# The attention gate's sums moved beside the convolutions, the feed forward gate's into its first projection

## The chip, the cores and the metric

One Trainium2 chip; the kernel runs on one core of it. The metric is the device time of one execution in microseconds (us). The core's engines are TensorE (PE, with its weight loads as PEld), VectorE (DVE), ScalarE (ACT), GpSimd (POOL) and SyncE (SP). Each engine runs its own instructions in a fixed order and waits on semaphores where an operand isn't ready; SP, ACT and POOL also issue DMAs.

## The reference

A transformer block for 512 tokens of width 2048 whose shifts, scales and gates come from a vector c through one wide weight (adaptive layer norm). Cut to what matters here:

```python
sh_a, sc_a, g_a, sh_f, sc_f, g_f = split(silu(c) @ ada_w + ada_b, 6)   # six rows of 2048
h = modulate(rms_norm(x, norm_mix), sh_a, sc_a)
...                                                # convolutions and attention -> y (512 x 2048)
x = x + g_a * (y @ w_out)                          # the output projection, gated
h = modulate(rms_norm(x, norm_ffn), sh_f, sc_f)
x = x + g_f * ((silu(h @ ffn_w1) * (h @ ffn_w3)) @ ffn_w2)
```

g_a is the attention's gate and g_f the feed forward's. Each is 2048 numbers, each number a product of c with a column of ada_w (2048 x 12288, float32).

## The kernel before

**The sums.** A row such as g_a is computed on DVE, 512 columns at a time. ada_w's 2048 rows lie as 16 tiles of 128 partitions x 512 columns (256 KB each). `ada` (L184) goes over them: it loads tiles (L195, on SP), and for each adds tile times one number per partition to a running sum `acc` (L201, one scalar_tensor_tensor). For the gates `acc` starts at zero (L190, a memset on POOL) with the bias in its first partition (L191, a DMA on SP). Then `quarters` (L219) sums `acc` over the partitions with four small matmuls, and the row goes to DRAM by `row_of` (L228, a DMA on POOL), to `gad` for the attention's gate and `gfd` for the feed forward's. `ada_bcast` (L230) does this and loads the row back to all 128 partitions as the tile `ga`. `ffn_part` (L466) computes one 512-column part of what the feed forward needs: parts 0 to 7 are its shifts and scales, 8 to 11 its gate.

**Where the sums stand.** `gates_beside` (L1002) yields the tiles that run beside the convolutions: parts 3 to 10, then the first 512 columns of g_a, nine parts of 16 tiles. The output projection (y @ w_out) is done in four blocks of 512 output columns. A block is eight steps; a step loads a tile of w_out (`raw`, L91, on SP), splits it into a high part `whi` (L92, ACT) and a low part `wlo` (L93, DVE), and makes 24 matmuls with it (L110 to L112, three for each product), six into each of four PSUM tiles of 128 tokens. `beside_block` (L1075) runs beside each block: it sends the block's gate through `ada_bcast`, and computes the next block's 512 columns of g_a (beside the last block, part 11, the last of g_f). `residual` (L1092) closes a block: for each of the four PSUM tiles t = tile times gate (L1096), x2 = x2 + t (L1097), a square on ACT (L1098), and DMAs of the result on POOL (L1102). L1096 empties the PSUM tile, and the next block's first matmul into it waits for that. `after_taken` lets the sums of a block be issued only after the residual's last add.

**The feed forward's first projection** multiplies by w1 and w3 in products of a Strassen-like scheme, one unit of 128 columns in seven products, after two plain units (`NP8` = 8 products). For every product a weight tile is split (`w_hi` L1237 on ACT, `w_lo` L1244 on DVE), multiplied on PE (L1251, L1253) and added to its outputs on DVE (L1258, L1262). Some weight tiles are sums of two (L1349 on DVE, or a DMA on POOL that adds while it loads, L1227, onto what a DMA on SP brought, L1225). The main loop goes over `order`, the list of products, and prepares later ones ahead.

**The order on an engine** isn't that of the code: a scheduler places each instruction by its operands and its own estimate of times, so an instruction without open dependencies may be placed far ahead of where it is written. Once built, an engine's order is fixed.

Of the kernel before, what the change touches and what calls it, by code (L numbers as in the profile page):

```python
# [9 lines left out]
F32 = mybir.dt.float32  # L10
# [3 lines left out]
ALU = mybir.AluOpType  # L14
# [3 lines left out]
P = 128  # L18
D = 2048
S = 512  # L20
NT = S // P
KC = D // P
# [47 lines left out]
def block_kernel(ctx: ExitStack, tc: tile.TileContext, a: dict, out: bass.AP):  # L70
    nc = tc.nc
# [4 lines left out]
    def pool(name, bufs=1, stack=ctx, **kw):  # L76
        return stack.enter_context(tc.tile_pool(name=name, bufs=bufs, reuse_waits="tile", **kw))
# [61 lines left out]
    accp = pool("acc", 2)  # L139
# [9 lines left out]
    cT = cp.tile([P, KC], F32, name="cT")  # L149
# [3 lines left out]
    aring = pool("araw", 8, stack=st0)  # L153
# [29 lines left out]
    ada_v = ada_w.rearrange("(p k) n -> p k n", k=KC)  # L183

    def ada(ring, width, c0, n, got, bias=False):

        acc = accp.tile([P, 512], F32, tag="acc", name="acc")[:, :n]
        step = min(width // n, KC)
        if bias:
            nc.gpsimd.memset(acc, 0.0)  # L190
            nc.sync.dma_start(acc[0:1, :], a["ada_b"][:, c0:c0 + n])  # L191
        for k0 in range(0, KC, step):
            raw = ring.tile([P, width], F32, tag="araw", name="araw")
            rv = raw[:, :step * n].rearrange("p (k n) -> p k n", k=step)
            nc.sync.dma_start(rv, ada_v[:, k0:k0 + step, c0:c0 + n])  # L195
            for k in range(k0, k0 + step):
                w, s = rv[:, k - k0, :], cT[:, k:k + 1]
                if k == 0 and not bias:
                    nc.vector.tensor_scalar(acc, w, s, None, op0=ALU.mult)
                else:  # L200
                    nc.vector.scalar_tensor_tensor(acc, w, s, acc, op0=ALU.mult, op1=ALU.add)  # L201
            yield
        got.append(acc)
# [15 lines left out]
    def quarters(t):  # L219

        ps = aux()
        for j in range(4):
            nc.tensor.matmul(ps[32 * j:32 * j + 32, :P], ones[:, 0:32], t[:, j * P:(j + 1) * P], start=True, stop=True,
                             skip_group_check=True)
        return ps[:, :P]

    def row_of(row, t):
        nc.gpsimd.dma_start(row.rearrange("o (j t) -> (o j) t", j=4), t[0:P:32, :P])  # L228

    def ada_bcast(row, small, dst, acc):  # L230

        nc.scalar.copy(small, quarters(acc))
        row_of(row, small)
        nc.gpsimd.dma_start(dst, row.to_broadcast([P, 512]))
# [225 lines left out]
    gfd = dram.tile([1, D], F32, name="gfd")  # L460
    gad = [dram.tile([1, 512], F32, name=f"gad{n}") for n in range(4)]
    rsd = [dram.tile([1, S], F32, name=f"rsd{c}") for c in range(8)]

    def ffn_part(ring_, width, j):

        got = []  # L466
        if j < 8:
            m, j = 1 - j % 2, j // 2
            yield from ada(ring_, width, (3 + m) * D + j * 512, 512, got)
            ada_cols(aux, got[0], 1, m, 4 * j, 4)  # L470
        else:
            cs = slice((j - 8) * 512, (j - 7) * 512)
            yield from ada(ring_, width, 5 * D + cs.start, 512, got, bias=True)
            nc.scalar.copy(got[0][:, :P], quarters(got[0]))
            row_of(gfd[:, cs], got[0])
        yield

    def ffn_parts(ring_, width, js):
        for j in js:
            yield from ffn_part(ring_, width, j)  # L480
# [60 lines left out]
    for name, m, t0, t1, n in (("q", 0, 0, NT, P), ("c", 1, NT, NT + 1, NP_), ("s", 2, 0, NT, P), ("w", 3, 0, NT, P)):  # L541
        f = SCALE if name == "q" else 1.0
        for h in range(2):
# [6 lines left out]
                                           op0=ALU.mult, op1=ALU.mult)  # L550
# [437 lines left out]
        for c in range(8):  # L988
            yield from conv(c)

    acc_g = []

    class Places:
        n = 0
# [5 lines left out]

    def gates_beside():
        places = Places()  # L1002
        yield from ffn_parts(places, 512, range(3, 11))
        yield from ada(places, 512, 2 * D, 512, acc_g, bias=True)

    later = gates_beside()
    weave(beside(convs(), later, (0.4,) * 24 + (0.83,)), attention_steps(), 0.59 / 3)
# [20 lines left out]
    gst = ExitStack()  # L1028
    gp = pool("ga", 1, stack=gst)
    xp = pool("x2", 2, stack=gst)  # L1030
    tp = pool("tmp", 2, stack=gst)
    aring = pool("aring2", 3, stack=gst)
    keep = pool("keep", 1, stack=gst)
    ss2 = gp.tile([P, NT, 4], F32, name="ss2")
    x2s = [None] * 4
# [27 lines left out]
        x2s[n] = xp.tile([P, NT, 512], F32, tag="x2", name="x2")  # L1063
        nc.sync.dma_start(x2s[n], x[:, n * 512:(n + 1) * 512].rearrange("(i p) n -> p i n", p=P))

    taken = [None]

    def after_taken(side):
        while True:
            with tc.issue_after(taken[-1]) if taken[-1] else ExitStack():  # L1070
                if next(side, side) is side:
                    return
            yield

    def beside_block(n, ga):  # L1075

        own = acc_g[-1]
        side = ffn_part(aring, 1024, 11)
        if n < 3:
            side = ada(aring, 1024, 2 * D + (n + 1) * 512, 512, acc_g, bias=True)  # L1080
        for t, _ in enumerate(after_taken(side)):
            if t == 0:
                if n:
                    x2_turned(n - 1)
                ada_bcast(gad[n], tp.tile([P, P], F32, tag="dg", name="dg"), ga, own)
                if 0 < n < 3:
                    x_load(n + 1)
            if n == 0 and t in (2, 5):
                x_load(t // 3)
            yield  # L1090

    def residual(n, ga, pst, tiles):  # L1092
        for i in tiles:
            t = tp.tile([P, 512], F32, tag="t", name="t")
            x2 = x2s[n][:, i, :]
            nc.vector.tensor_mul(t, pst[i], ga)  # L1096
            taken[-1] = nc.vector.tensor_add(x2, x2, t).ins  # L1097
            nc.scalar.activation(t, x2, AF.Square, accum_out=ss2[:, i, n:n + 1])  # L1098
        for i in tiles[::2]:
            to = xd[n] if n < 2 and i else \  # L1100
                out[0, i * P:(i + 2) * P, n * 512:(n + 1) * 512].rearrange("(i p) n -> p i n", p=P)
            nc.gpsimd.dma_start(to, x2s[n][:, i:i + 2, :])  # L1102
# [76 lines left out]
    for n in range(4):  # L1179
        ga = tp.tile([P, 512], F32, tag="ga", name="ga")  # L1180
# [238 lines left out]
    for u in range(PLAIN, NU):  # L1419
# [9 lines left out]
        else:  # L1429
            order += new[2:-1]  # L1430
            late = new[-1]

    begun = set()

    def begin(u):
# [23 lines left out]
    for n in range(3):  # L1459
        prepare(n, "split")  # L1460
    for n, s in enumerate(order):
        for m in range(n + 5, n + 1, -1):
            if m < len(order) and lead[id(order[m])] == m - n:
                prepare(m, "sum")
        if n == 0:
            for m in range(5, NP8):
                order[m]["load"]()
        for m in (n + 6, n + 7) if n < NP8 else (n + 7,):
            if m < len(order) and (n >= NP8 or m < NP8 + 1):
                begin(order[m]["u"])  # L1470
        if n > 2:
            prepare(n + 2, "split")
            h_sums(n)
        if n == len(order) - 5:
            zst.close()
            krp = pool("kraw", 1, side="right")
            for half in range(2):
                k_load(0, half)
        if n == 2:
            second_half()  # L1480
            h_sums(0)
        s["mm"](s)
        if n == 2:
            prepare(3, "split")
            h_sums(2)
            prepare(4, "split")
            with tc.issue_after(hi_ins[-1]):
                shifted(8, 8)
                shifted(0, 8)
        if n + 1 < len(order):  # L1490
            s["post"](s)
# [262 lines left out]
```

## Time and profile before

| | |
|---|---|
| three runs | 2167.26, 2167.44, 2171.16 us, median 2167.44 |
| profiled execution, its own time | 2169.3 us |
| its span | 2167.5 us |
| granted TensorE clock | 0.999 |

The times below come from the profiled execution, counted from the start of its span. The convolutions and the attention come first, the output projection lies from about 686 to 872 us, the first projection of the feed forward from 871 to about 1740, and the second from there to the end. A row of a timeline gives the start and the duration in us, the engine, the line, the operation, output and inputs with their shapes, how many were joined into the row, and in brackets the idle time ahead of it with what ended that. In a row of groups the bar is followed by the busy time in us, the mean duration of one in ns, and the idle time ahead of the group.

### The profile page before, as it was taken

The numbers are of one execution on the slowest core, as the hardware profiler recorded it, in microseconds if no ns is written. First come the engines' busy times: TensorE is split into PE (matmuls) and PEld (weight loads), VectorE is DVE, ScalarE is ACT, GpSimd is POOL, SyncE is SP. The second block draws the span as 40 slices with busy tenths as digits, with TensorE's granted clock in tenths as the row PEclk, the third lists the DMA queues.
The fourth block names the chain that finished last, engine by engine and source line by source line (L and its number), as shares of the span: only waits on it lengthen the run. The fifth ranks groups of instructions, "written<-read, shape, count | busy, mean of one in ns | idle before, by whom it ended". The sixth has DMA issues, their size and how long they took to land.

```text
span 2167.5 us, 30927 instructions
## 1 busy us (share of the span) xinstructions
PE 2137.4 (99%) x11501; PEld 1792.0 (83%) x11501; DVE 1720.6 (79%) x2562; ACT 1004.2 (46%) x1613; POOL 222.5 (10%) x273
## 2 busy tenths in 40 slices
PE   7999999999999999999999999999999999999999
PEld 5778778788788888888888888888888887888887
DVE  6788779877876656988878887888788887878788
ACT  5325244555555223744444444444444455444543
POOL 2310000000000100000000000000000122111210
PEclk9999999999999999999999999999999999999999
DMA  9975768745644975397777777777776499797975
GB/s 353 363 238 167 248 198 272 224 146 158 182 142 149 307 266 171 93 230 181 173 189 173 170 172 181 177 174 167 177 184 167 112 302 288 147 305 140 287 159 142
DMA packets 442219, 437.61 MB, mean 202 GB/s; under 512 B 20420, under 2 KB 349164, under 8 KB 441428
## 3 DMA queue, kind: packets, MB, share of 16 engines
q1 hardware_dynamic: 373088, 326.71, 48.2%
q0 software_dynamic: 68448, 108.44, 24.2%
q8 instruction: 90, 1.47, 0.3%
q14 instruction: 61, 0.50, 0.1%
q10 hardware_dynamic: 532, 0.48, 0.1%
HBM read 415.61 MB, written 19.96 MB: 201 GB/s over the span
## 4 chain that ended last, share of the span: by engine, by line
PE 88%; DVE 5%; DMA 5%; issue 1%; ACT 1%; SPq 0%; POOL 0%; DVEq 0%; ACTq 0%
PE main L1251 15%; PE aux L1251 11%; PE aux L1609 9%; PE main L1609 9%; PE main L1253 8%; PE main L110 7%; PE main L112 6%; PE main L111 6%; PE aux L1253 6%; DMA araw<-in_ada_w 2%; PE aux L110 2%; PE aux L112 2%; PE aux L111 2%; PE aux L902 2%; DVE acc L201 1%
## 5 line engine op out<-in xcount | busy, mean ns | idle before, releaser
L1237 ACT CAST whi<-raw 128x1024 fp32r<-128x1024 f32 x246 | 257.7, 1047 | 286.4 <-PE main L1251 95.7
L1251 PE MATMUL main<-hC,whi 128*128 128x512 f32 x1408 | 353.5, 392 | 1.4 <-ACT whi L1237 1.4
L1237 ACT CAST whi<-t 128x1024 fp32r<-128x1024 f32 x186 | 195.3, 1051 | 263.3 <-PE aux L1251 70.3
L1244 DVE TENSOR_TENSOR wlo<-raw,whi 128x1024 fp32r<-128x1024 f32 x218 | 265.9, 1220 | 54.5 <-ACT whi L1237 52.1
L1251 PEld LDWEIGHTS main<-hC,whi 128*128 128x128 f32 x1408 | 253.3, 189 | 47.6 <-ACT whi L1237 1.6
L1251 PE MATMUL aux<-hC,whi 128*128 128x512 f32 x1072 | 268.9, 392 | 0.0
L1251 PEld LDWEIGHTS aux<-hC,whi 128*128 128x128 f32 x1072 | 192.9, 189 | 34.4
L1253 PEld LDWEIGHTS main<-hC,wlo 128*128 128x128 f32 x1408 | 192.0, 190 | 13.6
L1253 PE MATMUL main<-hC,wlo 128*128 128x256 f32 x1408 | 196.4, 282 | 0.0
L110 PE MATMUL main<-alo,whi 128*128 128x512 f32 x444 | 179.7, 405 | 0.7 <-DVE rq L564 0.7
L112 PE MATMUL main<-ahi,whi 128*128 128x512 f32 x444 | 174.0, 393 | 0.0
L111 PE MATMUL main<-ahi,wlo 128*128 128x512 f32 x444 | 173.8, 391 | 0.0
L92 ACT CAST whi<-raw 128x1024 fp32r<-128x1024 f32 x70 | 73.6, 1052 | 189.9 <-PE main L112 122.7
L1253 PEld LDWEIGHTS aux<-hC,wlo 128*128 128x128 f32 x1072 | 146.3, 190 | 10.4
L1253 PE MATMUL aux<-hC,wlo 128*128 128x256 f32 x1072 | 149.7, 282 | 0.0
L1581 DVE TENSOR_TENSOR wlo<-t,whi 128x1024 fp32r<-128x1024 f32 x102 | 124.2, 1220 | 29.1 <-ACT whi L1237 29.0
L1227 POOL DMA_DIRECT2D t<-in_ffn_w x42 | 64.9, 1546 | 794.6 <-DVE d L1258 571.4
L1244 DVE TENSOR_TENSOR wlo<-t,whi 128x1024 fp32r<-128x1024 f32 x84 | 102.6, 1221 | 37.4 <-ACT whi L1237 36.2
L93 DVE TENSOR_TENSOR wlo<-raw,whi 128x1024 fp32r<-128x1024 f32 x70 | 85.2, 1219 | 44.2 <-ACT whi L92 44.1
L1258 DVE TENSOR_TENSOR d<-aux,d 128x256 f32<-128x256 f32 x168 | 70.8, 421 | 62.3 <-PE aux L1253 62.2
L1609 PE MATMUL aux<-whi,glo 128*128 128x512 f32 x308 | 119.8, 389 | 0.0
L1609 PE MATMUL aux<-whi,ghi 128*128 128x512 f32 x308 | 119.8, 389 | 0.0
(370 smaller groups left out, 4302.9 us busy)
## 6 DMA issues: line engine op xcount, KB each, us to landing
raw<-in_ffn_w SPq DMA_DIRECT2D x204, 512.0 KB, 5.0
t<-in_ffn_w POOLq DMA_DIRECT2D x90, 512.0 KB, 7.6
t<-in_ffn_w SPq DMA_DIRECT2D x78, 512.0 KB, 4.5
araw<-in_ada_w POOLq DMA_DIRECT2D x56, 512.0 KB, 13.6
kT<-in_ada_w SPq DMA_DIRECT2D x100, 256.0 KB, 4.2
raw<-in_w_in SPq DMA_DIRECT2D x128, 192.0 KB, 2.7
araw<-in_ada_w SPq DMA_DIRECT2D x40, 512.0 KB, 6.9
raw<-in_w_in SPq DMA_DIRECT2D x38, 512.0 KB, 4.1
```

Source lines behind the costliest of these rows:

```text
L92: nc.scalar.copy(hi[:, :m], raw[:, :m])
L93: nc.vector.tensor_sub(lo[:, :m], raw[:, :m], hi[:, :m].bitcast(F32))
L110: nc.tensor.matmul(ps, lhs[0], rhs[1], start=first, stop=False)
L111: nc.tensor.matmul(ps, lhs[1], rhs[0], start=False, stop=False)
L112: nc.tensor.matmul(ps, lhs[0], rhs[0], start=False, stop=last)
L1237: hi_ins[-1] = nc.scalar.copy(hi, t).ins
L1244: lo_ins[-1] = nc.vector.tensor_sub(lo, t, hi.bitcast(F32)).ins
L1251: nc.tensor.matmul(ps, wt[0][:, ks[k]], hc(p, k), start=first and k == 0, stop=False, skip_group_check=True)
L1253: nc.tensor.matmul(ps[:, HS:], wt[1][:, ks[k]], hc(p, k)[:, 0:HS], start=False, stop=last and k == HK - 1, skip_group_check=True)
L1258: nc.vector.tensor_add(to, ps[:, h * HS:(h + 1) * HS], to)
L1581: W["last"] = nc.vector.tensor_sub(lo, t, hi.bitcast(F32)).ins
L1609: nc.tensor.matmul(ps[2 * t + c], x_[:, j, tok], w[:, cs], start=m == 0 and j == 0 and p in (1, 5, 2), stop=m == 2 and j == GS[b] - 1 and ...
```

## The change

All four parts of g_a are now computed beside the convolutions (`gate_row`, each sent to `gad` there), after parts 3 to 7 of the feed forward; that is again nine parts. Nothing is summed at the output projection by the code: `beside_block` only loads its gate row from `gad`. All four parts of g_f come from `gate_sums`, which the main loop of the first projection calls before every third product from product 22 on; a call takes one tile's sum and issues the next tile's load. It has one tile for the loads, `gf_raw`, and one sum, `gf_acc`, made when `gate_sums` first runs, and its loads are on POOL. The diff:

```diff
-    acc_g = []
+    def gate_row(ring_, n):
+        got = []
+        yield from ada(ring_, 512, 2 * D + n * 512, 512, got, bias=True)
+        nc.scalar.copy(got[0][:, :P], quarters(got[0]))
+        row_of(gad[n], got[0])
+        yield
...
     def gates_beside():
         places = Places()
-        yield from ffn_parts(places, 512, range(3, 11))
-        yield from ada(places, 512, 2 * D, 512, acc_g, bias=True)
+        yield from ffn_parts(places, 512, range(3, 8))
+        for n in range(4):
+            yield from gate_row(places, n)
...
-    aring = pool("aring2", 3, stack=gst)
...
-    taken = [None]
-
-    def after_taken(side):
-        while True:
-            with tc.issue_after(taken[-1]) if taken[-1] else ExitStack():
-                if next(side, side) is side:
-                    return
-            yield
-
     def beside_block(n, ga):
 
-        own = acc_g[-1]
-        side = ffn_part(aring, 1024, 11)
-        if n < 3:
-            side = ada(aring, 1024, 2 * D + (n + 1) * 512, 512, acc_g, bias=True)
-        for t, _ in enumerate(after_taken(side)):
+        nc.gpsimd.dma_start(ga, gad[n].to_broadcast([P, 512]))
+        for t in range(9):
             if t == 0:
                 if n:
                     x2_turned(n - 1)
-                ada_bcast(gad[n], tp.tile([P, P], F32, tag="dg", name="dg"), ga, own)
...
-            taken[-1] = nc.vector.tensor_add(x2, x2, t).ins
+            nc.vector.tensor_add(x2, x2, t)
...
+    def gate_sums():
+        raw = accp.tile([P, 512], F32, tag="acc", name="gf_raw")
+        acc = accp.tile([P, 512], F32, tag="acc", name="gf_acc")
+        for c0 in range(0, D, 512):
+            nc.gpsimd.memset(acc, 0.0)
+            nc.sync.dma_start(acc[0:1, :], a["ada_b"][:, 5 * D + c0:5 * D + c0 + 512])
+            for k in range(KC):
+                nc.gpsimd.dma_start(raw, ada_v[:, k, 5 * D + c0:5 * D + c0 + 512])
+                yield
+                nc.vector.scalar_tensor_tensor(acc, raw, cT[:, k:k + 1], acc, op0=ALU.mult, op1=ALU.add)
+            nc.scalar.copy(acc[:, :P], quarters(acc))
+            row_of(gfd[:, c0:c0 + 512], acc)
+            yield
+
+    sums = gate_sums()
...
     for n, s in enumerate(order):
+        if n >= NP8 + 14 and n % 3 == 0:
+            next(sums, None)
```

In the changed kernel the lines behind this move up: the residual is L1088 to L1094, the accumulating load L1219, the split L1236, the takes L1250 and L1254, the sum of weights L1341; in `gate_sums` the memset is L1429, the load L1432 and the sum L1434.

How the instructions stand. First DVE, at the end of block 0 of the output projection, before: splits (wlo) and sums of the second part of g_a (acc_6902), down to the first product of block 0's residual.

```order
L93 TENSOR_TENSOR wlo_7024<-raw_7022,whi_7023 128x1024
L201 SCALAR_TENSOR_TENSOR acc_6902<-araw_7018,cT_82,acc_6902 128x512 x2
L201 SCALAR_TENSOR_TENSOR acc_6902<-araw_7052,cT_82,acc_6902 128x512 x2
L93 TENSOR_TENSOR wlo_7058<-raw_7056,whi_7057 128x1024
L201 SCALAR_TENSOR_TENSOR acc_6902<-araw_7086,cT_82,acc_6902 128x512 x2
L93 TENSOR_TENSOR wlo_7094<-raw_7092,whi_7093 128x1024
L201 SCALAR_TENSOR_TENSOR acc_6902<-araw_7122,cT_82,acc_6902 128x512 x2
L201 SCALAR_TENSOR_TENSOR acc_6902<-araw_7156,cT_82,acc_6902 128x512 x2
L93 TENSOR_TENSOR wlo_7128<-raw_7126,whi_7127 128x1024
L93 TENSOR_TENSOR wlo_7185<-raw_7183,whi_7184 128x1024
L93 TENSOR_TENSOR wlo_7257<-raw_7255,whi_7256 128x1024
L1096 TENSOR_TENSOR t_7160<-main_6868,ga_6867 128x512
```

The same place of DVE in the changed kernel, from the third sum of the first 512 columns of g_f on (two sums, L1434, stand further ahead, one before and one behind a split).

```order
L1434 SCALAR_TENSOR_TENSOR gf_acc_8972<-gf_raw_8971,cT_82,gf_acc_8972 128x512 x2
L93 TENSOR_TENSOR wlo_7031<-raw_7029,whi_7030 128x1024
L1434 SCALAR_TENSOR_TENSOR gf_acc_8972<-gf_raw_8971,cT_82,gf_acc_8972 128x512
L93 TENSOR_TENSOR wlo_7063<-raw_7061,whi_7062 128x1024
L1434 SCALAR_TENSOR_TENSOR gf_acc_8972<-gf_raw_8971,cT_82,gf_acc_8972 128x512 x2
L93 TENSOR_TENSOR wlo_7093<-raw_7091,whi_7092 128x1024
L1434 SCALAR_TENSOR_TENSOR gf_acc_8972<-gf_raw_8971,cT_82,gf_acc_8972 128x512
L93 TENSOR_TENSOR wlo_7146<-raw_7144,whi_7145 128x1024
L1434 SCALAR_TENSOR_TENSOR gf_acc_8972<-gf_raw_8971,cT_82,gf_acc_8972 128x512 x2
L93 TENSOR_TENSOR wlo_7203<-raw_7201,whi_7202 128x1024
L1088 TENSOR_TENSOR t_7121<-main_6872,ga_6871 128x512
L1088 TENSOR_TENSOR t_7125<-main_6873,ga_6871 128x512
```

The sums of the first part of g_f, which the code calls from product 22 of the first projection on, stand here, ten of them ahead of the residual; the eleventh stands behind the second add of the residual and ahead of its third product, the twelfth to sixteenth behind the residual, between the splits of block 1. All ten read the one tile gf_raw_8971. Before, the last sum stood three splits ahead of the residual and each had one of three tiles.

Next POOL at the same place, before: the load of the normalisation row cc and of the gate ga, accumulating loads of the first projection (t2), and the stores of block 0.

```order
L977 DMA cc_6758<-rsd7_1737 128x512
L234 DMA ga_6867<-gad0_1726 128x512
L1227 DMA t2_8287<-in_ffn_w3 128x8x128
L1102 DMA out_0<-x2_6986 128x2x512
L1227 DMA t2_8729<-in_ffn_w3 128x8x128
L1102 DMA xd0_6795<-x2_6986 128x1024
```

And in the changed kernel:

```order
L1073 DMA ga_7139<-gad1_1727 128x512
L228 DMA rsd7_1737<-u_3041 4x128
L1432 DMA gf_raw_8971<-in_ada_w 128x512
L977 DMA cc_6765<-rsd7_1737 128x512
L1432 DMA gf_raw_8971<-in_ada_w 128x512 x2
L1219 DMA t2_8112<-in_ffn_w3 128x8x128
L1432 DMA gf_raw_8971<-in_ada_w 128x512
L1219 DMA t2_8553<-in_ffn_w3 128x8x128
L1432 DMA gf_raw_8971<-in_ada_w 128x512 x6
L1094 DMA out_0<-x2_6967 128x2x512
```

POOL now issues the loads of gf_raw there, one for each sum, in one queue with the accumulating loads and the stores; the two gates ga of blocks 0 and 1 are loaded ahead of them.

Last, DVE in a unit of the first projection, before: splits (L1244), takes (L1258) and a sum of weights (L1349).

```order
L1244 TENSOR_TENSOR wlo<-raw,whi 128x1024
L1258 TENSOR_TENSOR d_12305<-aux,d_12305 128x256
L1244 TENSOR_TENSOR wlo<-raw,whi 128x1024
L1258 TENSOR_TENSOR d_12305<-aux,d_12305 128x256
L1258 TENSOR_TENSOR d_12281<-aux,d_12281 128x256
L1244 TENSOR_TENSOR wlo<-t_12251,whi 128x1024
L1258 TENSOR_TENSOR d_12281<-aux,d_12281 128x256
L1349 TENSOR_TENSOR t_12251<-t_12251,raw 128x1024
L1258 TENSOR_TENSOR d_12305<-main,d_12305 128x256
L1244 TENSOR_TENSOR wlo<-raw,whi 128x1024
L1258 TENSOR_TENSOR d_12305<-main,d_12305 128x256
```

The same stretch of a unit in the changed kernel, from one sum of g_f's second part to the next.

```order
L1434 SCALAR_TENSOR_TENSOR gf_acc_8972<-gf_raw_8971,cT_82,gf_acc_8972 128x512
L1250 TENSOR_TENSOR d2_10407<-aux_10390,d2_10407 128x256
L1236 TENSOR_TENSOR wlo_10485<-raw_10349,whi_10483 128x1024
L1250 TENSOR_TENSOR d2_10407<-aux_10390,d2_10407 128x256
L1250 TENSOR_TENSOR d1_10381<-aux_10487,d1_10381 128x256
L1236 TENSOR_TENSOR wlo_10509<-t2_10351,whi_10507 128x1024
L1250 TENSOR_TENSOR d1_10381<-aux_10487,d1_10381 128x256
L1341 TENSOR_TENSOR t2_10351<-t2_10351,raw_10354 128x1024
L1250 TENSOR_TENSOR d2_10407<-main_10364,d2_10407 128x256
L1236 TENSOR_TENSOR wlo_10545<-raw_10170,whi_10543 128x1024
L1250 TENSOR_TENSOR d2_10407<-main_10364,d2_10407 128x256
L1434 SCALAR_TENSOR_TENSOR gf_acc_8972<-gf_raw_8971,cT_82,gf_acc_8972 128x512
```

The rest is as it was; three sums were put into each unit, the third five rows behind the second one shown. Parts 2 to 4 of g_f stand like this, each over some five units, and their `quarters` on PE come more than a unit behind the last sum.

## The prediction

> **What bounds the kernel now.** I read the page's busy shares first, then the busy time of two stretches of the span (the output projection, and a piece of the feed forward's first projection), then the waits of PE.
>
> ```profile
> span 2167.5 us, 30927 instructions
> PE 2137.4 (99%) x11501; PEld 1792.0 (83%) x11501; DVE 1720.6 (79%) x2562; ACT 1004.2 (46%) x1613; POOL 222.5 (10%) x273
> ...
> 690.00:872.00 182.00, 181.84 (x863) 149.34 (x862) 110.23 (x146) 57.27 (x94) 15.93 (x23) 1.00 0.74 241
> 1200.00:1395.50 195.50, 195.50 (x1122) 172.06 (x1121) 157.97 (x211) 90.53 (x131) 15.40 (x10) 1.00 0.73 175
> ```
>
> The two long rows give a stretch, its length, then the busy time of PE, PEld, DVE, ACT and POOL, the granted clock, the DMA share and GB/s. PE is busy 181.84 of 182.00 us in the output projection and 195.50 of 195.50 in the first projection, at clock 1.00. So PE's own matmuls are the time, and work taken off DVE, POOL or the queues shortens nothing unless PE waited for it. What PE does wait for from the sums in the output projection is one place:
>
> ```profile
> 755.62 3.11 DVE L201 SCALAR_TENSOR_TENSOR acc<-araw,cT,acc 128x512 f32<-128x512 f32 x4 [7.10 <-DMA araw<-in_ada_w]
> 758.65 1.22 DVE L93 TENSOR_TENSOR wlo<-raw,whi 128x1024 fp32r<-128x1024 f32 x1
> ...
> 759.92 0.50 PE L110 MATMUL main<-wlo,ahi 128*128 128x512 f32 x1 [0.16 <-DVE wlo L93]
> ```
>
> Four sums (L201) waited 7.10 us for their tile; the split of the next weight tile (wlo, L93) stands behind them in DVE's order, and PE waited 0.16 us for it. This is the mechanism to keep in mind: **a sum that waits for a DMA holds whatever stands behind it on DVE.** Before, only one such wait reached PE. So the most that the change can gain by emptying the output projection is the 182.00 - 181.84 = 0.16 us there, half a microsecond at the outside.
>
> **The change, part by part.** *Work on PE.* Eight sums of 512 columns are turned by `quarters` before and after (three beside the convolutions and five at the output projection; then four and four), so PE's own work is unchanged. *Beside the convolutions* there are nine parts of 16 tiles before and after: 0. *The output projection* loses its 64 L201 sums and their loads on SP, worth at most the 0.16 us above.
>
> *The feed forward's gate* is 64 sums on one tile, gf_raw. Its next load is issued on POOL only when the sum before it has read it, so the sums are a serial loop: sum, release to POOL, load, sum. The order shown above tells where it runs. Only columns 2 to 4 stand in the feed forward. **The 16 sums of column 1 stand in blocks 0 and 1 of the output projection**, on DVE ahead of weight splits and, for ten of them, ahead of the residual of block 0 (L1096 before, L1088 after). PE's first matmuls of block 1 need that residual, since it empties their PSUM. What one turn of the loop costs:
>
> ```profile
> L201 DVE SCALAR_TENSOR_TENSOR acc<-araw,cT,acc 128x512 f32<-128x512 f32 x109 | 81.7, 749 | 34.4 <-DMA araw<-in_ada_w 32.8
> ...
> 690.17 0.95 DVE L136 RECIPROCAL u<-u 128x128 f32<-128x128 f32 x1
> ...
> 691.41 0.54 POOL L228 DMA_DIRECT2D rsd<-u  x1 [27.95 <-DVE u L136]
> ```
>
> A sum is 0.75 us. POOL issued its DMA at 691.41 after DVE had ended at 691.12: 0.3 us for the release. No 256 KB load of ada_w by POOL is in this trace, so its landing is bounded by the rows of other 256 KB loads (last number: median us from issue to landing).
>
> ```profile
> kT<-in_ada_w SPq DMA_DIRECT2D x100, 256.0 KB, 4.2
> araw<-in_ada_w SPq DMA_DIRECT2D x48, 256.0 KB, 3.1
> k<-gd POOLq DMA_DIRECT2D x44, 256.0 KB, 7.0
> cc<-rsd POOLq DMA_DIRECT2D x8, 256.0 KB, 5.2
> ga<-gad POOLq DMA_DIRECT2D x4, 256.0 KB, 5.8
> ...
> DMA to landing us min/median/max: 2.9/7.0/12.4
> ```
>
> From below: 2.9, the shortest of the 44 loads of k (last row, the line that issues them; most of those queue behind one another). From above: 5.8, ga, issued by POOL in this very stretch, but from one short row for all partitions. I take **3.8**, the mean of the first two rows weighted by count (148 loads of the same tile shape from the same weight, on SP), since they are nearest in what they read. One turn is then T = 0.75 + 0.3 + 3.8 = 4.85 us, between 3.95 and 6.85.
>
> Now DVE's rows of before around the border of blocks 0 and 1, and PE's at it:
>
> ```profile
> 693.76 3.11 DVE L201 SCALAR_TENSOR_TENSOR acc<-araw,cT,acc 128x512 f32<-128x512 f32 x4
> 701.52 0.75 DVE L984 SCALAR_TENSOR_TENSOR yc<-yc,cols,cc 128x512 f32<-128x512 f32 x1 [4.66 <-DMA cc<-rsd]
> ...
> 725.85 1.23 DVE L93 TENSOR_TENSOR wlo<-raw,whi 128x1024 fp32r<-128x1024 f32 x1 [4.21 <-ACT whi L92]
> 726.99 1.28 DVE L1096 TENSOR_TENSOR t<-main,ga 128x512 f32<-128x512 f32 x2
> ...
> 729.77 0.39 PE L112 MATMUL main<-whi,alo 128*128 128x512 f32 x1
> 730.00 0.39 PE L110 MATMUL main<-wlo,ahi 128*128 128x512 f32 x1
> ```
>
> Block 1 starts on PE at 730.00; the residual's first product starts at 726.99 and takes half of 1.28, so it is ready 2.4 us early. In the changed order: sums 1 and 2 come before L984, whose tile cc lands at 701.5 as before (its row of DMAs waits for nothing new but the second load). Behind L984 stand one split (1.14, from 725.85 to 726.99) and two short casts (0.7), so sum 3 starts at 701.5 + 0.7 + 1.1 + 0.8 = 704.1. Sum 10 follows seven turns later, 704.1 + 7T; the splits between them fit into the waits. Behind sum 10: its 0.75, one split 1.14, the first product 0.68, which ends at 706.7 + 7T. With T = 4.85 that is 740.6 against 730.0: PE stands 10.6 us. The third product stands behind sum 11 and ends at 704.1 + 8T + 0.75 + 0.69, while PE needs it 2.7 us (12 matmuls of 0.23) after the first: T - 3.85 more, 1.0. Sum: 8T - 27.2 = **11.6 us**. Sums 12 to 16 stand before splits of block 1 that PE needs late; they add nothing up to T = 5.3 (sum 16 is six turns behind sum 10, and the split behind it is due 29.6 us into block 1), and 5T - 26.4 above. At the lower end, T = 3.95, the total is 4.4; at the upper, 6.85, it is 27.6 + 7.9 = 35.5.
>
> *Columns 2 to 4.* In the first projection a unit of seven products, 19.55 us, holds three sums. Its DVE is busy 157.97 of 195.50 us, 3.75 idle a unit; three sums take 2.25, so it fits.
>
> ```profile
> 1306.12 1.22 DVE L1244 TENSOR_TENSOR wlo<-t,whi 128x1024 fp32r<-128x1024 f32 x1
> 1307.26 0.41 DVE L1258 TENSOR_TENSOR d<-aux,d 128x256 f32<-128x256 f32 x1
> 1307.59 1.21 DVE L1349 TENSOR_TENSOR t<-t,raw 128x1024 f32<-128x1024 f32 x1
> 1308.72 0.42 DVE L1258 TENSOR_TENSOR d<-main,d 128x256 f32<-128x256 f32 x1
> ```
>
> From start to start a split (L1244) or a sum of weights (L1349) is 1.14, a take (L1258) 0.33. By the order there stand six takes and four such (6.5 us) between the first and second sum of a unit, two and three (4.1) between the second and third, and 4.7 from the third to the next unit's first; with the sum itself 7.2, 4.8 and 5.4, so a turn of 4.85 is hidden, the shortest gap within some tenths that the unit's idle time gives; two turns and 7.2 exceed the unit only above T = 6.2. I cost it at 0. The cover is the loop being shorter than DVE's own work; if it goes, each 0.1 us of T costs 0.2 a unit, over some 16 units, less a lead of a few microseconds that the splits have in each column. The last sum of each column comes well over a unit ahead of its `quarters` on PE, so no wait there.
>
> **The rivals.** *Not slower:* the load is short. The stall needs 8T - 27.2 > 0, and within 0.2% of the time (4.3 us, about what a measurement of this kernel tells from no change) it stays if T < 3.95, that is a landing under 2.9 us at each of eight turns. Against it: one row of 44 is that short, and this stretch moves 241 GB/s. For it: as DVE stalls, SP's loads stall too and the queue empties. Time: 2167.4 to 2171.7. [...] The trace speaks against it so far, with 2.9 as the least and medians of 5.2 to 7.0.
>
> *Longer still:* landings of 5.8 and more, as ga. Then both the first block's stall (35.5 us) and the first projection's loop (at T = 6.85, 1.35 us a unit, some 7 a column less its lead) come out: 2200 to 2215.
>
> *As named:* the sums run in the first projection only and the output projection is free. Then DVE there is 92% busy, still under PE, and the time is 2167, a gain of 0.2 us at best. The order says otherwise for column 1. That the time falls by more than 4.3 us would need PE waits that the trace doesn't have.
>
> **How the numbers follow.** The profiled execution of before took 2169.3 us by its own time (span 2167.5), 1.9 above the median of 2167.44; 2169.3 + 11.6 = 2180.9 there, and 2167.4 + 11.6 = 2179.0 against the median. Forecast (a stall of 4.4 to 30 us at the border of blocks 0 and 1): 79%. Not slower: 10%. Longer still: 6%. As named: 3%. Faster by something that I don't see: 2%. The forecast's bounds are 2171.8 and 2203; the range runs from 2169.5, into the not-slower case, to 2198, T = 6.5. Faster by over 0.2%: 0.03; within: 0.14; slower: 0.83.
>
> **What would show it.** In the changed profile: PE idle of about 10 us at one place near 730 to 741, released by DVE's product of the residual (L1088), and 1 us soon after; DVE waiting for gf_raw before nearly every L1434 there, starts of L1434 4.85 us apart; POOL's loads of gf_raw landing in 3.8 us; PE without waits in the first projection. Wrong would be: starts under 4 us apart and no such wait; sums that DVE runs in another order than shown; PE waiting in the first projection for splits; or a change of PE's own busy time.

## The result, and the profile after

| | before | changed |
|---|---|---|
| median of 6 runs | 2167.47 us (2166.44 to 2171.16) | 2181.40 us (2179.86 to 2183.31) |
| ratio | | 1.0062, 95% interval 1.0052 to 1.0073 |
| span of the profiled execution | 2167.5 us | 2178.4 us |

The change made the kernel 13.9 us slower, by the medians; 11.6 were forecast, and a time of 2179.0. The two profiled executions took 2169.3 and 2180.1 us by their own times, 10.8 apart: the one before lay above its median, the changed one below it. First the page's busy time, and the two stretches of the span that the prediction began with: length, then busy time of PE, PEld, DVE, ACT and POOL, granted clock, DMA share, GB/s.

```profile
span 2178.4 us, 30998 instructions
PE 2140.1 (98%) x11501; PEld 1793.8 (82%) x11501; DVE 1713.4 (79%) x2562; ACT 1005.3 (46%) x1613; POOL 258.0 (12%) x337
```

```profile
690.00:872.00 182.00, 170.67 (x759) 140.55 (x759) 66.05 (x83) 47.85 (x73) 18.79 (x29) 0.97 0.53 163
1200.00:1395.50 195.50, 195.50 (x1133) 171.58 (x1132) 168.39 (x230) 91.57 (x132) 28.15 (x32) 1.00 0.80 202
```

PE is idle for 182.00 - 170.67 = 11.3 us of the output projection, where it was idle for 0.16; in the first projection it is as full as before, though DVE there rose from 157.97 to 168.39 us. Two things in the first of these rows are to be seen: the idle time, and a granted clock of 0.97 where it was 1.00. PE waits there at three places, twice for a split (4.2 us) and once for the residual of block 0 (7.1 us). Its rows at those places (start, duration, idle ahead in brackets):

```profile
713.30 0.50 PE L110 MATMUL main<-wlo,ahi 128*128 128x512 f32 x1 [2.67 <-DVE wlo L93]
...
727.64 0.50 PE L110 MATMUL main<-wlo,ahi 128*128 128x512 f32 x1 [1.55 <-DVE wlo L93]
...
740.49 0.79 PE L110 MATMUL main<-wlo,ahi 128*128 128x512 f32 x1 [7.10 <-DVE t L1088]
741.08 0.63 PE L111 MATMUL main<-whi,ahi 128*128 128x512 f32 x1
741.50 0.63 PE L112 MATMUL main<-whi,ahi 128*128 128x512 f32 x1
...
744.71 0.40 PE L111 MATMUL main<-whi,ahi 128*128 128x512 f32 x1
744.94 0.39 PE L112 MATMUL main<-whi,ahi 128*128 128x512 f32 x1
```

The idle times add up to 2.67 + 1.55 + 7.10 = 11.3 us. Behind the longest, matmuls start 0.42 us apart (741.08 to 741.50), three us later 0.23 apart again (744.71 to 744.94). Two windows of that piece, before and after 744.5, say why:

```profile
740.40:744.20 3.80, 3.71 (x9) 2.94 (x10) 3.80 (x8) 2.27 (x5) 1.28 (x2) 0.50 0.67 238
745.00:749.00 4.00, 4.00 (x25) 3.44 (x24) 1.43 (x2) 2.03 (x5) 0.54 (x1) 1.00 0.79 221
```

The granted clock was 0.50 in the first window, 3.8 us from the restart on, and 1.00 in the second, from 745 on. The clock fell behind the idle of 2.67 us as well:

```profile
710.28:713.69 3.41, 0.74 (x4) 0.35 (x3) 1.89 (x2) 1.04 (x1) 1.29 (x2) 1.00 1.18 154
713.69:717.11 3.42, 3.42 (x10) 2.65 (x9) 1.53 (x2) 0.00 (x0) 1.35 (x2) 0.50 0.84 236
```

PE was idle for 2.67 of the first 3.41 us, at clock 1.00, and the clock was 0.50 throughout the next 3.42, although PE was busy in all of it. Now DVE, whose order is that shown under the change:

```profile
704.96 0.75 DVE L1434 SCALAR_TENSOR_TENSOR gf_acc<-gf_raw,cT,gf_acc 128x512 f32<-128x512 f32 x1
711.36 0.75 DVE L1434 SCALAR_TENSOR_TENSOR gf_acc<-gf_raw,cT,gf_acc 128x512 f32<-128x512 f32 x1 [5.65 <-DMA gf_raw<-in_ada_w]
712.03 1.22 DVE L93 TENSOR_TENSOR wlo<-raw,whi 128x1024 fp32r<-128x1024 f32 x1
715.58 0.75 DVE L1434 SCALAR_TENSOR_TENSOR gf_acc<-gf_raw,cT,gf_acc 128x512 f32<-128x512 f32 x1 [2.33 <-DMA gf_raw<-in_ada_w]
...
721.73 0.75 DVE L1434 SCALAR_TENSOR_TENSOR gf_acc<-gf_raw,cT,gf_acc 128x512 f32<-128x512 f32 x1 [4.26 <-DMA gf_raw<-in_ada_w]
725.70 0.75 DVE L1434 SCALAR_TENSOR_TENSOR gf_acc<-gf_raw,cT,gf_acc 128x512 f32<-128x512 f32 x1 [3.23 <-DMA gf_raw<-in_ada_w]
...
737.95 0.75 DVE L1434 SCALAR_TENSOR_TENSOR gf_acc<-gf_raw,cT,gf_acc 128x512 f32<-128x512 f32 x1 [3.26 <-DMA gf_raw<-in_ada_w]
738.61 1.22 DVE L93 TENSOR_TENSOR wlo<-raw,whi 128x1024 fp32r<-128x1024 f32 x1
739.75 1.28 DVE L1088 TENSOR_TENSOR t<-main,ga 128x512 f32<-128x512 f32 x2
```

All of these sums but the first wait for their tile, and the split at 712.03 and the residual at 739.75 stand behind such waits. Sum 3 starts at 704.96, sum 10 at 737.95: seven turns of 4.7 us. The turns are of two kinds, though: 4.0 to 4.2 (711.36 to 715.58, 721.73 to 725.70) and 6.2 to 6.4 (704.96 to 711.36, 715.58 to 721.73). The loads' own line, with its landing times over all 64:

```profile
DMA to landing us min/median/max: 2.8/4.6/6.4
```

Where the loss arose shows in the starts of the same matmuls in both profiles (counted in PE's order, without those of `quarters`):

```
before us   changed us   difference
   694.4        691.2        -3.2
   722.3        723.7        +1.4     behind the idle at 713
   727.1        730.3        +3.2     behind the idle at 728
   732.5        744.9       +12.5     behind the idle at 740
   863.2        872.8        +9.6     end of the output projection
  1728.5       1740.3       +11.8     end of the first projection
  2135.0       2145.7       +10.8
```

The three stalls cost 4.6 + 1.85 + 9.2 = 15.7 us, 4.3 more than the idle times. The -3.2 ahead of them isn't the change's doing for certain: in the six profiles below that keep the attention gate's move, it was anything from -3.2 to +0.2. The step from +12.5 to +9.6 and back to +11.8 is mostly `quarters` gone from one stage to the other, some 0.55 us each.

### The profile page after: what moved, and what is told of

It reads as the page before. It is cut to its first block, busy times and chain, and to the rows that moved or that the text cites. A ratio compares the mean times of both kernels' runs of the same rounds, so it can differ in the third digit from the quotient of the medians.

```text
span 2178.4 us, 30998 instructions
## 1 busy us (share of the span) xinstructions
PE 2140.1 (98%) x11501; PEld 1793.8 (82%) x11501; DVE 1713.4 (79%) x2562; ACT 1005.3 (46%) x1613; POOL 258.0 (12%) x337
## 4 chain that ended last, share of the span: by engine, by line
PE 64%; DMA 1%; DVE 1%; issue 0%; ACT 0%; POOL 0%; DVEq 0%; ACTq 0%
PE main L1243 15%; PE aux L1243 11%; PE aux L1618 9%; PE main L1618 9%; PE main L1245 8%; PE aux L1245 6%; PE main L110 2%; PE main L111 2%; PE main L112 2%; DMA k<-gd 1%; DMA gf_raw<-in_ada_w 1%; PE aux L1052 0%; DVE wlo L1590 0%; DVE glo L1544 0%; PE aux L1061 0%
## 5 line engine op out<-in xcount | busy, mean ns | idle before, releaser
L1236 DVE TENSOR_TENSOR wlo<-raw,whi 128x1024 fp32r<-128x1024 f32 x218 | 266.2, 1221 | 49.0 <-ACT whi L1229 47.6
L1245 PEld LDWEIGHTS aux<-hC,wlo 128*128 128x128 f32 x1072 | 146.2, 190 | 10.4
L1236 DVE TENSOR_TENSOR wlo<-t,whi 128x1024 fp32r<-128x1024 f32 x84 | 102.6, 1222 | 25.1 <-ACT whi L1229 25.1
L1219 POOL DMA_DIRECT2D t<-in_ffn_w x42 | 65.8, 1566 | 474.1 <-DVE d L1250 324.0
L1618 PE MATMUL aux<-wlo,ghi 128*128 128x512 f32 x308 | 119.7, 389 | 0.0
```

The costliest lines, as they stand in the source:

```text
L1219: nc.gpsimd.dma_start(b["t"].rearrange("p (k n) -> p k n", k=HK), block(u, 12), accum_op=ALU.add)
L1236: lo_ins[-1] = nc.vector.tensor_sub(lo, t, hi.bitcast(F32)).ins
L1245: nc.tensor.matmul(ps[:, HS:], wt[1][:, ks[k]], hc(p, k)[:, 0:HS], start=False, stop=last and k == HK - 1, skip_group_check=True)
L1618: nc.tensor.matmul(ps[2 * t + c], x_[:, j, tok], w[:, cs], start=m == 0 and j == 0 and p in (1, 5, 2), stop=m == 2 and j == GS[b] - 1 and ...
```

## The experiments

Timed runs were compared with the kernel before on the same chip.

**The sums held in the first projection.** Each call is issued behind the last split given to DVE:

```diff
-            next(sums, None)
+            with tc.issue_after(lo_ins[-1]):
+                next(sums, None)
```

> The changed kernel with one edit: each call of the gate's sums is issued behind the weight split that DVE has just been given, so that no sum of the feed forward's gate can stand in the output projection; all 64 stand in the first projection. Theory (the loss is the first column's serial loop ahead of block 0's splits and residual, and the slow matmuls after its stalls): PE has no wait at blocks 0 and 1, and the time goes back to that of before, 2165 to 2169 us. Rival (the serial loop on one tile costs wherever it stands): PE waits for splits in the first projection, some 1 us a unit over 27 units, 2185 us or more. Rival (the attention gate's four rows beside the convolutions cost): still 2175 or more.

2169.57 us against 2167.78, ratio 1.0007 (0.9999 to 1.0016). The stretch of the output projection, and the sums' line (count, durations in ns, first and last start):

```profile
690.00:872.00 182.00, 182.00 (x842) 151.72 (x840) 67.27 (x86) 57.78 (x94) 12.36 (x17) 1.00 0.49 151
```

```profile
L1434 DVE SCALAR_TENSOR_TENSOR gf_acc<-gf_raw,cT,gf_acc x64: 736/743/753, 969.7 to 1525.4; 128x512 f32<-128x512 f32 x64
```

All 64 sums now lie between 969.7 and 1525.4, PE is never idle in the output projection, its clock stays at 1.00, and the loss is gone, to within the interval. The time is 0.6 us above the range that was expected. In the first projection the one tile and its serial loop cost 0.8 us in this profile (one wait, told below): the loss lies in the place.

**One load for each column.** The first of 16 tiles is read by all 16 sums:

```diff
+                if k == 0:
-                nc.gpsimd.dma_start(raw, ada_v[:, k, 5 * D + c0:5 * D + c0 + 512])
+                    nc.gpsimd.dma_start(raw, ada_v[:, k, 5 * D + c0:5 * D + c0 + 512])
```

> The changed kernel, but only the first of each column's 16 tiles is loaded and all 16 sums read it (leaves out 15 of 16 tiles of the feed forward's gate). The sums keep their number and may stand as early as before; what goes is the wait for a load between one and the next. Theory (the wait in the serial loop): no PE wait near 710, 726 and 733, 2165 to 2169 us. Rival (the sums' own work on DVE ahead of the residual, ten times 0.75 us): 7.5 us of DVE work remain ahead of the residual, less 2.4 us of lead, 2171 to 2174 us.

2166.78 us, ratio 0.9996 (0.9987 to 1.0005). The sums still stand in block 0, and PE was busy 182.00 of 182.00 us there. But their order isn't that of the changed kernel. DVE's rows of the last four sums, the next splits and the residual:

```profile
709.23 3.11 DVE L1435 SCALAR_TENSOR_TENSOR gf_acc<-gf_raw,cT,gf_acc 128x512 f32<-128x512 f32 x4
712.26 2.35 DVE L93 TENSOR_TENSOR wlo<-raw,whi 128x1024 fp32r<-128x1024 f32 x2
...
723.79 1.28 DVE L1088 TENSOR_TENSOR t<-main,ga 128x512 f32<-128x512 f32 x2
```

All 16 sums were done by 712.3, and four splits stand between the last of them and the residual, where the changed kernel has one split behind sum 10. So this run shows that 12 us of the sums' work fit into block 0 without a wait of PE; what ten sums would cost without loads in the places that the changed kernel gives them, it doesn't show. That the waits for the loads are the cause rests on this and on DVE's rows of the changed kernel, where the idle time ahead of the sums ends with the loads.

**No loads and no sums.**

```diff
             for k in range(KC):
-                nc.gpsimd.dma_start(raw, ada_v[:, k, 5 * D + c0:5 * D + c0 + 512])
                 yield
-                nc.vector.scalar_tensor_tensor(acc, raw, cT[:, k:k + 1], acc, op0=ALU.mult, op1=ALU.add)
```

> The changed kernel without the loads and sums of the feed forward's gate (leaves out that gate's product; its bias, the turning by PE and the stores remain). It shows what the rest of the change is worth: the attention gate's four rows beside the convolutions and the emptied output projection. Theory: the rest is worth nothing, 2165 to 2168 us, within 1 us of the kernel whose sums are held in the first projection. Rival (64 sums in the first projection cost DVE time that PE waits for): this one is 3 us or more faster than that kernel.

2167.33 us, ratio 0.9996 (0.9987 to 1.0005): moving the attention gate and emptying the output projection are worth nothing, as the 0.16 us of PE idle there had said. It is 2.2 us below the held kernel, and nine of the held kernel's eleven runs lie above all eleven of these. By the starts of the same matmuls the first projection grew by 3.1 us against the kernel before in the held profile and by 2.2 here, where its four `quarters` alone account for it. The 0.8 us between them are one wait of PE in the held kernel, at a column's `quarters`; the two profiles differ by another 0.7 us ahead of the output projection, and what causes that is open.

**The loads on SP.**

```diff
-                nc.gpsimd.dma_start(raw, ada_v[:, k, 5 * D + c0:5 * D + c0 + 512])
+                nc.sync.dma_start(raw, ada_v[:, k, 5 * D + c0:5 * D + c0 + 512])
```

> The changed kernel with the loads of gf_raw issued on SP in place of POOL, still one tile. By its order five sums, not ten, stand ahead of block 0's residual. Theory (turns of the loop counted ahead of the residual): five turns of some 4.5 us from 694 end by 717, well ahead of 727, and no more than one sum stands between two splits: no stall, 2165 to 2171 us. Rival (a load that waits for a sum now holds SP's queue, and so the weight tiles behind it): PE waits for whi or wlo late in blocks 0 and 1, 2175 us or more.

2179.41 us, ratio 1.0051 (1.0039 to 1.0064). The theory's number was missed and the rival's hit. PE waited 3.1 us for a split and 3.5 for the residual. DVE's timeline:

```profile
691.13 0.75 DVE L1434 SCALAR_TENSOR_TENSOR gf_acc<-gf_raw,cT,gf_acc 128x512 f32<-128x512 f32 x1 [0.39 <-DMA gf_raw<-in_ada_w]
...
716.16 0.75 DVE L1434 SCALAR_TENSOR_TENSOR gf_acc<-gf_raw,cT,gf_acc 128x512 f32<-128x512 f32 x1 [8.25 <-DMA gf_raw<-in_ada_w]
...
736.67 0.75 DVE L1434 SCALAR_TENSOR_TENSOR gf_acc<-gf_raw,cT,gf_acc 128x512 f32<-128x512 f32 x1 [2.82 <-DMA gf_raw<-in_ada_w]
737.34 0.68 DVE L1088 TENSOR_TENSOR t<-main,ga 128x512 f32<-128x512 f32 x1
```

and SP's own:

```profile
694.44 0.57 SPq L1217 DMA_DIRECT2D t<-in_ffn_w  x1
706.11 0.37 SPq L91 DMA_DIRECT2D raw<-in_w_out  x1
706.53 0.46 SPq L1217 DMA_DIRECT2D t<-in_ffn_w  x1
707.05 1.80 SPq L1432 DMA_DIRECT2D gf_raw<-in_ada_w  x1
```

The second load was free to go at 692, but it stands on SP behind a weight tile that had to wait for its buffer until 706, and went out at 707. Sum 2 came at 716. There were also seven sums ahead of the residual, not the five that I counted. So it isn't POOL as such: on SP, too, the serial load inherits what stands ahead of it, and the residual inherits the load. The rival's mechanism isn't in this trace: from 685 to 775, ACT's casts of the weight tiles (whi) waited for PE, one more for 1.4 us without a cause that the profile names, and none for its tile.

```profile
ACT whi L92 <- PE main L112: 36.9, 10, 4.4
```

**Every second load.** Two sums for each load:

```diff
+                if k % 2 == 0:
-                nc.gpsimd.dma_start(raw, ada_v[:, k, 5 * D + c0:5 * D + c0 + 512])
+                    nc.gpsimd.dma_start(raw, ada_v[:, k, 5 * D + c0:5 * D + c0 + 512])
```

> The changed kernel with a load for every second sum only (leaves out every second tile of the feed forward's gate). Fifteen sums stand ahead of or inside block 0's residual and eight loads, where the changed kernel has eleven sums and eleven loads there. Theory (the number of load turns sets when the residual comes): five turns of 4.8 to 7 us behind the sum at 705 bring the first product of the residual to about 736, against 740.4, so PE stands some 4 us less there, and the time is 2175 to 2178 us. Rival (the number of sums ahead of the residual): four more sums, 2184 us or more.

2187.56 us, ratio 1.0089 (1.0076 to 1.0103): slower than the changed kernel, against the theory. The number would fit the rival, but the trace names another cause. POOL's timeline, and then DVE's:

```profile
711.75 3.26 POOL L1219 DMA_DIRECT2D t<-in_ffn_w  x2
716.24 0.59 POOL L1433 DMA_DIRECT2D gf_raw<-in_ada_w  x1 [1.22 <-DVE gf_acc L1435]
```

```profile
725.29 1.54 DVE L1435 SCALAR_TENSOR_TENSOR gf_acc<-gf_raw,cT,gf_acc 128x512 f32<-128x512 f32 x2 [8.21 <-DMA gf_raw<-in_ada_w]
```

With half the loads, the two accumulating loads t came to stand side by side ahead of one load of gf_raw. It was issued at 716.24 and read at 725.29, a landing of 9.0 us; the load just ahead, issued at 711.23, had taken 3.1. The four more sums are 3 us of DVE work; this one wait is 8.21. PE stood idle for 8.2 us at a split and 6.2 at the residual. A count of turns isn't enough: what each stands behind has to be read from the queue.

**The accumulating loads behind block 0.** They are issued on POOL after block 0's stores; DVE's order is unchanged:

```diff
-            nc.gpsimd.dma_start(to, x2s[n][:, i:i + 2, :])
+            stored[-1] = nc.gpsimd.dma_start(to, x2s[n][:, i:i + 2, :]).ins
+            if n == 0:
+                stored[0] = stored[-1]
...
+                with tc.issue_after(stored[0]):
-                nc.gpsimd.dma_start(b["t"].rearrange("p (k n) -> p k n", k=HK), block(u, 12), accum_op=ALU.add)
+                  nc.gpsimd.dma_start(b["t"].rearrange("p (k n) -> p k n", k=HK), block(u, 12), accum_op=ALU.add)
```

> The changed kernel with the first projection's accumulating loads (t, 512 KB each, on POOL) issued behind the stores of block 0. DVE's order stays, the ten sums ahead of the residual too; what goes is that two of those loads stand between the loads of gf_raw in POOL's queue. Theory (a turn of the loop takes 4.1 us where the load of gf_raw is alone on POOL's queue, and 6.2 where it stands behind another load): from the third sum, near 705, seven turns of 4.1 bring sum 10 to about 734 in place of 738, the splits of the fifth step come in time or within 1 us, and the whole time is 2174 to 2178 us. Rival (the landing of gf_raw depends on the traffic of all queues, not on what stands ahead of it on POOL): turns stay at 4.7 us on average, 2180 to 2183.

2186.14 us, ratio 1.0084 (1.0071 to 1.0098): a miss in the total, though not for the rival's reason. The turn that had stood behind such a load fell from 6.2 to 4.2 us; the one from sum 3 to 4, which I had put down to them too, stayed at 6.3. It may have to do with the traffic of other queues (SP issued two loads of 512 KB at 704.93 and 705.35), but no run shows that apart. So sum 10 came at 736.6, not the 734 expected and 1.4 us earlier than in the changed kernel, and PE still waited 7.2 us for the residual: by the starts of the same matmuls block 0 still lost 14.1 us, with six turns of 4.0 to 4.3 us and the one of 6.3. The two loads then met the sums of block 1. POOL and DVE there:

```profile
744.76 3.21 POOL L1224 DMA_DIRECT2D t<-in_ffn_w  x2
749.24 0.59 POOL L1437 DMA_DIRECT2D gf_raw<-in_ada_w  x1 [1.26 <-DVE gf_acc L1439]
```

```profile
762.87 0.75 DVE L1439 SCALAR_TENSOR_TENSOR gf_acc<-gf_raw,cT,gf_acc 128x512 f32<-128x512 f32 x1 [12.79 <-DMA gf_raw<-in_ada_w]
767.09 0.75 DVE L1439 SCALAR_TENSOR_TENSOR gf_acc<-gf_raw,cT,gf_acc 128x512 f32<-128x512 f32 x1 [3.47 <-DMA gf_raw<-in_ada_w]
767.75 1.22 DVE L93 TENSOR_TENSOR wlo<-raw,whi 128x1024 fp32r<-128x1024 f32 x1
```

One load behind both took 13.5 us to land, DVE waited 12.79 us for it, and PE 4.0 us for the split behind it. The wait was moved, not removed.

**One idle time by itself.** To measure the slow matmuls without the sums, the kernel before got a product computed one, four or twelve times more, which holds block 0's residual:

```diff
     def residual(n, ga, pst, tiles):
+        if n == 0:
+            t = tp.tile([P, 512], F32, tag="t", name="t")
+            for _ in range(1):                          # 4, 12
+                held = nc.vector.tensor_mul(t, pst[3], ga).ins
         for i in tiles:
...
+            with tc.issue_after(held) if n == 0 else ExitStack():
+                nc.vector.tensor_mul(t, pst[i], ga)
```

> The kernel before, with one product of block 0's last PSUM tile and its gate computed once more on DVE, ahead of the residual of block 0. It holds the residual until PE has ended the block, so that PE stands idle once, for about 1.7 us near 730. Theory (the matmuls run at half the clock for some 3.5 us after an idle of 2.7 us or more, as they did at 713 and 741 in the changed kernel, and not after 1.7 us): matmuls start every 0.23 us right after the idle, and PE lies 1.7 us behind the kernel before from there on. Rival (any idle that long slows the matmuls behind it): starts every 0.43 us, 3.3 us behind.

> The same with four such products ahead of the residual, so that PE stands idle for about 4.6 us near 730. Theory: some eight matmuls behind the idle start every 0.43 us, granted clock 0.5, and PE lies 4.6 + 1.7 = 6.3 us behind. Rival (the slow matmuls in the changed kernel came from DVE or the queues, not from the idle): starts every 0.23 us, 4.6 behind.

> The same with twelve such products, so that PE stands idle for about 9.5 us near 730. Theory: the slow stretch is as long as after the shorter idle, some eight matmuls and 1.7 to 2 us lost, 11.3 us behind in all. Rival (the slow stretch grows with the idle): 4 us lost or more, over 13 us behind.

PE's rows of the first, and the window behind its idle time:

```profile
731.37 0.50 PE L110 MATMUL main<-wlo,ahi 128*128 128x512 f32 x1 [1.38 <-DVE t L1101]
731.70 0.40 PE L111 MATMUL main<-whi,ahi 128*128 128x512 f32 x1
731.94 0.39 PE L112 MATMUL main<-whi,ahi 128*128 128x512 f32 x1
```

```profile
731.30:734.10 2.80, 2.73 (x12) 2.28 (x13) 2.80 (x5) 1.34 (x4) 1.30 (x3) 1.00 0.90 144
```

the second:

```profile
733.50 0.80 PE L110 MATMUL main<-wlo,ahi 128*128 128x512 f32 x1 [4.57 <-DVE t L1101]
734.09 0.63 PE L111 MATMUL main<-whi,ahi 128*128 128x512 f32 x1
734.51 0.63 PE L112 MATMUL main<-whi,ahi 128*128 128x512 f32 x1
```

```profile
733.40:738.30 4.90, 4.80 (x11) 3.84 (x12) 4.71 (x9) 2.21 (x7) 0.97 (x3) 0.50 1.32 249
```

and the third:

```profile
738.67 0.79 PE L110 MATMUL main<-wlo,ahi 128*128 128x512 f32 x1 [10.36 <-DVE t L1101]
```

```profile
738.60:743.80 5.20, 5.13 (x12) 4.06 (x13) 4.98 (x9) 2.54 (x8) 1.13 (x2) 0.50 0.26 101
```

| idle, us | slow matmuls behind it | clock there | PE behind, us | of it beyond the idle |
|---|---|---|---|---|
| 1.38 | none | 1.00 | 1.7 | 0.3 |
| 4.57 | 11 | 0.50 | 7.3 | 2.7 |
| 10.36 | 12 | 0.50 | 13.2 | 2.9 |

(PE behind: from the starts of the same matmuls, with the difference ahead of the idle taken off.) No sum and no load of a gate was changed here, so the slow matmuls follow from PE's idle time alone. They don't grow with it: twice the idle time brings one matmul more. They were more than expected, 11 and 12 where I had said eight, so PE lay 7.3 and 13.2 us behind where 6.3 and 11.3 were expected (0.9 of the last is the longer idle); the rival's loss of 4 us or more didn't come either. Times of these three, one run each: 2169.94, 2174.98 and 2179.75 us.

In the changed kernel an idle time of 2.67 us was enough: the clock was 0.50 behind it and behind that of 7.10 us, and 1.00 behind that of 1.55. How long the matmuls stayed slow doesn't follow the idle time, by their starts: 3.4 us behind the idle of 2.67 (713.63 to 716.98), 4.0 behind 7.10 (740.49 to 744.47), 5.3 behind 4.57 (733.50 to 738.76) and 5.3 behind 10.36 (738.67 to 743.96). Nor does the length of an idle time decide by itself whether the clock falls. Among the first matmuls PE was idle for 1.36 us ahead of 32.34 in the kernel before and ahead of 32.40 in the changed one. The same window behind it, before first:

```profile
33.71:37.12 3.41, 3.41 (x10) 2.63 (x9) 3.34 (x7) 0.55 (x2) 1.47 (x2) 0.50 1.02 315
```

```profile
33.71:37.12 3.41, 3.41 (x31) 2.74 (x31) 3.38 (x6) 1.21 (x3) 1.54 (x3) 1.00 0.91 305
```

The clock was 0.50 in the one and 1.00 in the other. What decided it no run shows.

None of the kernels that compute the whole beat the one before; held in the first projection, the change is level with it.

## Why the prediction was right

**Place and mechanism.** The first column's sums stand in blocks 0 and 1, and their waits held the residual of block 0: PE waited 7.1 us for L1088, the wait named ahead of time, at 733 to 740. With the sums held in the first projection the loss went; with the loads gone and the sums left, though placed further ahead, it went as well. Both halves of "a sum that waits for a DMA holds what stands behind it" are thus shown, the place by the first run, the wait by DVE's rows and the second run together.

**The size of the idle time.** 11.6 us were forecast, 11.3 came, by errors that cancel. A turn was put at 4.85 us and was 4.7 on average, but as a mix: some 4.1 in five turns (the load landed in 2.8 to 3.1 us, near the lower bound of 2.9) and 6.2 to 6.4 in two, one behind an accumulating load and one whose cause is open. The 3.8 us taken from SP's loads was a mean that few turns had. The idle time also was at three places, not one: "the splits between them fit into the waits" failed at 713 and 728, where PE stood 2.67 and 1.55 us for splits behind a sum. PE also came to the border of the blocks 3.2 us earlier than in the profile of before, which the sum couldn't know and which lengthens the idle time, and the restart and slow matmuls behind 713 and the restart at 728 used up 2.2 us of it. So that the total came within 0.3 us is luck; that it was some ten microseconds at this place is not. The microsecond for the third product didn't come: the tile of sum 11 landed while DVE still made the adds, and PE, at half clock, needed the product only at 745.2. One slip in the forecast itself: its stall of "4.4 to 30 us" and its upper bound of 2203 don't belong together, 2203 being a stall of 35.5; the result is far from both.

**What the sum lacked.** The three stalls cost 15.7 us, 4.3 more than PE's idle time. The restart behind the idle of 1.55 us cost 0.3 us, at clock 1.00, and behind the idle of 2.67 and of 7.10 us PE ran some eight matmuls at a granted clock of 0.50, 0.43 us apart in place of 0.23. The runs with one idle time by itself show this term apart: 2.7 to 2.9 us for an idle of 4.6 or 10.4, 0.3 for one of 1.4. The medians' 13.9 lies between the idle time and the 15.7: other parts of the run differ by some microseconds from one execution to the next, as the -3.2 to +0.2 above show.

**The rivals.** *Not slower* needed landings under 2.9 us at each turn. The five short turns came close to that; the two long ones, with landings of 5.0 and 5.3 us, were far from it. The lower end of the range, 2169.5, is a stall of 2.1 us, which takes a landing of 2.6 us; that was the author's estimate, and no run shows it: the least was 2.8 here, 2.7 with the loads on SP and 2.9 with every second load. *Longer still* did not come: PE has no wait in the first projection that the kernel before didn't have. *As named* is what the held kernel does, and its time, level with before within the interval, is what that rival had said. The expected gain of the emptied output projection was 0.16 us, and the run without sums shows none.

## What to carry to other kernels

Read where a scheduler has put an instruction before counting on where the code has it; here one edge that keeps the sums in their place undoes the loss. A load with one buffer, whose next turn waits for the last one's use, costs little (0.8 us here) where nothing urgent stands behind it on its engine, and a stall where a PSUM reader or a split does. Where PE will stand idle, add the restart and the clock to the idle time: in these runs 1.9 to 2.9 us beyond idle times of 2.67 to 10.36 us, and 0.3 beyond those of 1.38 and 1.55.

## What the runs showed of the hardware

At and behind the output projection's first block a PE idle of 1.38 or 1.55 us left the granted clock at 1.00; 2.67, 4.57, 7.10 and 10.36 us were followed by 0.50, for 3.4 to 5.3 us of the matmuls behind. Near 32 us an idle of 1.36 us was followed by 0.50 in the kernel before and by 1.00 in the changed one. Loads of 256 KB on POOL landed 2.8 to 3.1 us after their issue in the short turns, 9.0 and 13.5 us when issued 4.5 us behind the first of two accumulating loads of 512 KB on the same queue; such loads themselves landed in 6.3 to 11.0 us in the changed kernel, 7.8 in the median. Moving the accumulating loads in the queue moved the wait with them.
